# One attention kernel without softmax: TensorE's loop enlarged by a turn and put into one aligned block of program, stores reordered behind loads

## The chip, the cores and the metric

The kernel runs on one core of a Trainium2 chip. The metric is the device time of one execution in microseconds (us); lower is better. The time before is a median of three runs. A separate execution of the same kernel was taken with the hardware profiler, and its rows are what the prediction reads.

## The reference

Linear attention with a ReLU feature map. Q, K and V have 8 batches, 12 heads, 512 positions and 64 channels in float32.

```python
Q_feat = np.maximum(0, Q)
K_feat = np.maximum(0, K)
KV = np.einsum('bhkd,bhkv->bhdv', K_feat, V)
K_sum = np.sum(K_feat, axis=2)
numerator = np.einsum('bhqd,bhdv->bhqv', Q_feat, KV)
denominator = np.einsum('bhqd,bhd->bhq', Q_feat, K_sum)
out = numerator / (denominator[:, :, :, None] + 1e-10)
```

Each head needs a small 64x64 matrix KV and a vector K_sum, and every query row is multiplied with both. Three tensors of 12.58 MB are read and one of the same size is written.

## The kernel before, in words

The 96 heads are worked on in twelve groups of eight ("octets", `NO = 12`). One octet of Q, K or V is 1 MB in float32: 128 partitions with 32 rows of 64 numbers each, contiguous in HBM.

**Loads.** K and V of octet 0 come as float32 over the queues of SP and ACT (L94, L95) into `k8` and `v8`, which are the first two output buffers. Everything else is loaded by POOL (L96, L109), whose transfers turn float32 into bf16 on the way. K and V have a ring of `RING = 6` slots, Q has seven. Loads of octets 1 to 6 are issued at once; from octet 7 on POOL waits until the slot is free (`PR1`, `VC` and `STG`, L104 to L107).

**Stores.** An octet's result is written as float32 into one of `NOUT` buffers `o_sb` and stored by POOL (`store`, L114 to L117) once `NRM1` says that both halves are ready. Octets 10 and 11 are stored by SP. `HEAD = 4` sets how many stores stand between the loads in POOL's order: store 0 is issued ahead of the loads of octet 10, store 1 ahead of those of octet 11, and stores 2 to 9 behind all loads. Each store has a semaphore of its own, and at the end SP waits for all twelve and clears the semaphores (L317 to L321).

**Compute.** DVE prepares K (ReLU times a mask, L237) and V (L241, with ACT's share at L208), two halves g = 0 and 1 of an octet in `prep`, and copies Q (`stage`, L247). TensorE runs one `turn` for each octet, inside a loop (`Fori`, L189): it transposes Q (L158, sixteen), multiplies K with V (L167, 64 products), transposes the octet before back into rows (`back`, L148, sixteen in two halves), forms the denominators (L176) and the numerators (L184). The back transposes of an octet thus stand in the next turn, and those of octet 11 follow the loop as two more calls of `back` (L191 to L193). The loop's first instruction is aligned to the start of a block of 256 instruction slots by `head_slot` (L189). ACT applies ReLU to the transposed Q (L214), moves KV out of PSUM (L219) and the numerators (L228). DVE ends an octet with the denominators (L265 to L273) and `norm` (L259), which multiplies by the reciprocals and writes the output buffer.

**Order of DVE.** In pass o of its loop (L304 to L314): `prep(o+1, 0)`, `stage(o+1)`, `norm(o-1)`, `denominators(o)`, `prep(o+1, 1)`. The last `norm` follows the loop. Before the loop it makes masks and the columns of ones of `vo` with 18 memsets and three reductions (L275 to L300).

**Start.** Three barriers of all engines come ahead of the kernel's own text: one from the construction of the program (profile line L334) and two at L16 (`tc.close()` and `tc.compile()`). The first DMAs are issued behind the last one.

Of the kernel before, what the change touches and what calls it, by code (L numbers as in the profile page):

```python
# [5 lines left out]
def kernel(  # L6
# [5 lines left out]
):  # L12
    nc = tc.nc

    tc.close()
    tc.compile()  # L16

    B, H, S, D = Q.shape
    assert D == 64
    P = 128  # L20
    D1, D4 = D + 1, D + 4
    R = S * 4 // P
    RQ = 2 * R
    U = RQ // 2
    NO = B * H // 8
    assert NO * 8 == B * H and R == 16
    RING = 6
    NOUT = 9
    RUNS = (1,) * 11
    HEAD = 4  # L30

    fp32 = mybir.dt.float32
    bf16 = mybir.dt.bfloat16
    Act = mybir.ActivationFunctionType
    Alu = mybir.AluOpType
    PE, PL, VE, AC, SP = nc.tensor, nc.gpsimd, nc.vector, nc.scalar, nc.sync

    def view(X):
        return X.rearrange("b h s d -> (b h s d)").rearrange("(n p f) -> n p f", p=P, f=RQ * D)

    Qr, Kr, Vr, Or = view(Q), view(K), view(V), view(out)

    def sb(name, shape, dt):
        return nc.alloc_sbuf_tensor(name, shape, dt)[:]
# [3 lines left out]
    def sems(*names):  # L48
        new = [nc.alloc_semaphore(n) for n in names]
        handles.extend(new)  # L50
        return new

    ident = sb("ident", [P, P], bf16)
    ident32 = sb("ident32", [P, P], fp32)
    mask_k = sb("mask_k", [P, 2], fp32)
    mask_v = sb("mask_v", [P, 2], fp32)
    mask_h = sb("mask_h", [P, 8, 2], fp32)
    k_all = sb("k_all", [P, RING, RQ, D], bf16)
    v_all = sb("v_all", [P, RING, RQ, D], bf16)
    q_all = sb("q_all", [P, RING + 1, U * P], bf16)  # L60
    o_sb = [sb(f"o_sb{i}", [P, RQ, D], fp32) for i in range(NOUT)]
    k8, v8 = o_sb[0], o_sb[1]
# [1 line left out]
    q_sb = sb("q_sb", [P, U, P], bf16)  # L64
    qt_sb = sb("qt_sb", [P, U, P], bf16)
    kf = [sb(f"kf{i}", [P, R, 2, D], bf16) for i in range(2)]
    vo = [sb(f"vo{i}", [P, R, 2, D4], bf16) for i in range(2)]
    kvd = sb("kvd", [P, 8, 2 * D1], bf16)
    ot = sb("ot", [P, U, 8, 16], fp32)
    own = sb("own", [P, U, 8, 2], fp32)  # L70
# [10 lines left out]
    ID, STG, PR0, PR1, DEN, NRM0, NRM1, DV = sems(  # L81
        "id", "stg", "pr0", "pr1", "den", "nrm0", "nrm1", "dv")
    VC, KVD, OT = sems("vc", "kvd", "ot")
    CQ0, CQ1, CK0, CK1, CB0, CB1, CD, CO0, CO1 = sems(
        "cq0", "cq1", "ck0", "ck1", "cb0", "cb1", "cd", "co0", "co1")
    landed = {}
    stored = sems(*[f"st{o}" for o in range(NO)])

    def land(name):
        landed[name], = sems(name)  # L90
        return landed[name]
# [7 lines left out]
    def slot(o):  # L99
        return (o - 1) % RING if o > 0 else RING  # L100

    def load(o, n):
        last, to = o + n - 1 - RING, slot(o)
        for X, tile_, c, freed in ((Kr, k_all, "k", [PR1]), (Vr, v_all, "v", [VC, PR1]), (Qr, q_all, "q", [STG])):  # L104
            if last > 0:
                for s in freed:
                    PL.wait_ge(s, last + 1)  # L107
            t = tile_ if c == "q" else tile_.rearrange("p n r d -> p n (r d)")
            PL.dma_start(out=t[:, to:to + n], in_=X[o:o + n].rearrange("n p f -> p n f"),  # L109
                         single_packet=True).then_inc(land(f"{c}{o}"), 16)  # L110
        for i in range(o, o + n):
            run_of[i] = o

    def store(eng, o):  # L114
        eng.wait_ge(NRM1, o + 2)
        kw = {"single_packet": True} if eng is PL else {}
        eng.dma_start(out=Or[o], in_=o_sb[(o + 2) % NOUT].rearrange("p r d -> p (r d)"), **kw).then_inc(stored[o], 16)  # L117

# [4 lines left out]
    o, done = 1, 0  # L123
    for n in RUNS:
        while done < o + n - 1 - RING - HEAD + 1:
            store(PL, done)
# [11 lines left out]
    def arrived(eng, c, o):  # L138
        s = landed[f"{c}{run_of[o]}"]
        if (eng.engine, s.num) not in seen:  # L140
            seen.add((eng.engine, s.num))
            eng.wait_ge(s, 16)

    def back(j):
        for v in range(8):
            t = PE.transpose(ps_o[j][:, P * v:P * v + P], ot[:, 8 * j + v].rearrange("p h c -> p (h c)"), ident32)  # L148
        t.then_inc((CB0, CB1)[j], 1)
# [35 lines left out]
                              start=True, stop=True, skip_group_check=True)  # L185
            t.then_inc((CO0, CO1)[j], 1)

    PE.wait_ge(ID, 4)
    with nc.Fori(1, NO + 1, engines=bass.OrderedEngineSet([PE.engine]), head_slot={PE.engine: 0}) as i:  # L189
        turn(i)  # L190
    PE.wait_ge(OT, NO + 1)  # L191
    back(0)
    back(1)  # L193


    def v_rows(o, g):
        rows = slice(R * g, R * g + R)
        return v_all[:, slot(o), rows] if o > 0 else v8[:, rows]

    def k_rows(o, g):  # L200
        rows = slice(R * g, R * g + R)
        return k_all[:, slot(o), rows] if o > 0 else k8[:, rows]

    def v_scalar(o):
        arrived(AC, "v", o)
        if o == 0:
            AC.wait_ge(ID, 4)
        AC.activation(vo[0][:, :, 1, 2:D + 2], v_rows(o, 0), Act.Copy, scale=mask_v[:, 1:2]).then_inc(VC, 1)  # L208

    v_scalar(0)  # L210
    for o in range(NO):
        for j in range(2):
# [4 lines left out]
        for s in range(2):  # L217
            for c in range(2):
                t = AC.copy(  # L219
                    kvd[64 * c:64 * c + 64, s::2, c * D1:c * D1 + D1].rearrange("p (g t) d -> p g t d", t=2),  # L220
                    ps_kv[64 * s:64 * s + 64, :, 0:2 * (D + 2)].rearrange(
                        "p g (t d) -> p g t d", t=2)[:, :, :, c:c + D1])
# [3 lines left out]
        for j in range(2):  # L226
            AC.wait_ge((CO0, CO1)[j], o + 1)
            t = AC.copy(ot[:, :, 4 * j:4 * j + 4],  # L228
                        ps_o[j].rearrange("p (h u c) -> p u h c", h=4, u=U))
        t.then_inc(OT, 1)  # L230


    def prep(o, g):

        arrived(VE, "k", o)
        for s in range(2):
            VE.tensor_scalar(kf[g][:, :, s, :], k_rows(o, g), scalar1=0.0,  # L237
                             scalar2=mask_k[:, s:s + 1], op0=Alu.max, op1=Alu.mult)
        arrived(VE, "v", o)
        for t in range(1 + g):  # L240
            x = VE.tensor_scalar(vo[g][:, :, t, 2:D + 2], v_rows(o, g), scalar1=mask_v[:, t:t + 1],  # L241
                                 scalar2=None, op0=Alu.mult)
        x.then_inc((PR0, PR1)[g], 1)
# [5 lines left out]
    def norm(o):  # L249
        dst = o_sb[(o + 2) % NOUT]  # L250
        if o >= NOUT:
            VE.wait_ge(stored[o - NOUT], 16)
        VE.wait_ge(DV, 2 * o + 2 + DV0)
        if o == NOUT - 1:
            VE.wait_ge(VC, 1)
        for j in range(2):
            rs = slice(R * j, R * j + R)
            VE.wait_ge((CB0, CB1)[j], o + 2)
            VE.tensor_tensor(dst[:, rs], ps_o[j].rearrange("p (r d) -> p r d", d=D),  # L259
                             rec[o % 2][:, rs].unsqueeze(2).to_broadcast([P, R, D]),  # L260
                             op=Alu.mult).then_inc((NRM0, NRM1)[j], 1)

    def denominators(o):
# [7 lines left out]
                         op=Alu.add, axis=mybir.AxisListType.X).then_inc(DV, 1)  # L271
        VE.wait_ge(DV, 2 * o + 1 + DV0)
        VE.reciprocal(rec[o % 2], den).then_inc(DV, 1)  # L273

    for t in range(2):  # L275
        VE.memset(mask_v[:, t:t + 1], 0.0)
    VE.memset(kvd.rearrange("p h d -> p (h d)").bitcast(fp32), 0.0)
    VE.memset(ot.rearrange("p u h c -> p (u h c)"), 0.0).then_inc(OT, 1)
    ones = [vo[g][:, :, :, 1:D4 - 1][:, :, :, 0:D + 2:D1] for g in range(2)]
    VE.memset(ones[0], 0.0)  # L280
    VE.memset(ones[1], 0.0).then_inc(DV, 1)
    VE.wait_ge(DV, 1)
    for t in range(2):
        for half in range(2):
            b = 64 * half + 32 * t
            VE.memset(mask_v[b:b + 32, t:t + 1], 1.0)
            for g in range(2):
                VE.memset(ones[g][b:b + 32, :, t], 1.0)
    VE.wait_ge(ID, 2)
    VE.tensor_copy(ident32, ident).then_inc(ID, 1)  # L290
    VE.wait_ge(ID, 3)
    for c in range(2):
        VE.tensor_reduce(out=mask_h[:, :, c], in_=ident32.rearrange("p (h b) -> p h b", h=8),
                         op=Alu.add, axis=mybir.AxisListType.X)
    VE.tensor_reduce(out=mask_k, in_=ident32.rearrange("p (t s b) -> p s t b", t=4, s=2),
                     op=Alu.add, axis=mybir.AxisListType.XY).then_inc(ID, 1)
    DV0 = 1
    VE.wait_ge(ID, 4)
    for s in (DEN, NRM0, NRM1):
        VE.sem_inc(s, 1)  # L300
    prep(0, 0)
    prep(0, 1)
    stage(0)
    for o in range(NO):  # L304
        if o + 1 < NO:
            VE.wait_ge(CK0, o + 1)
            prep(o + 1, 0)
            stage(o + 1)
        if o > 0:
            norm(o - 1)  # L310
        denominators(o)
        if o + 1 < NO:
            prep(o + 1, 1)
    norm(NO - 1)  # L314


    for s in stored:  # L317
        SP.wait_ge(s, 16)
    used = sorted(s.num for s in handles)
    assert used == list(range(used[0], used[-1] + 1))  # L320
    SP.sem_clear(range(used[0], used[-1] + 1))  # L321
# [28 lines left out]
```

## Time and profile before

| what | us |
|---|---|
| median of three runs (124.69, 124.86, 125.21) | 124.86 |
| the profiled execution, its own time | 124.66 |
| its span | 123.4 |
| busy: DVE, PE, ACT, POOL | 89.3, 87.4, 79.4, 27.5 |
| first DMA issue (SP, L94) | 1.40 |
| last Q landed | 98.50 |
| last store issued (SP, L117) | 116.7 |
| HBM read and written | 37.75 MB and 12.58 MB |

The span runs from the first instruction of the program to the last, and the profiled execution's own time is 1.3 us longer than its span. Durations below come from this one execution. A loading DMA is counted with the bytes that it writes (bf16), half of what it reads. "PEclk" and the granted clock are the share of TensorE's full speed that the throttle granted. DMA shares over 1.00 are overlapping packets of one DMA engine.

### The profile page before, as it was taken

What the parts mean: (1) busy time and instruction counts of PE and PEld (TensorE: products, weight loads), DVE (VectorE), ACT (ScalarE), POOL (GpSimd) and SP (SyncE); (2) the same over time, 40 slices, a digit from 0 to 9 for tenths busy, and PEclk for the clock granted to TensorE, in tenths of its full rate; (3) what the DMA queues carried; (4) which work ended last, traced back from release to release, by engine and by line L of the source; (5) the groups of instructions that cost most, each with busy time, mean ns of one, the idle gap of its engine ahead of it and who ended that gap; (6) DMA issues with size and microseconds to landing.
All of it is one profiled execution on the core that took longest, in us unless ns stands there. A gap on an engine that the chain in (4) does not pass through costs nothing.

```text
span 123.4 us, 3380 instructions
## 1 busy us (share of the span) xinstructions
PE 87.4 (71%) x1456; PEld 75.9 (62%) x1456; DVE 89.3 (72%) x178; ACT 79.4 (64%) x109; POOL 27.5 (22%) x50
## 2 busy tenths in 40 slices
PE   0000099998998979799897998979449939977400
PEld 0000099986886868688686877958429928947200
DVE  3737906599989899998989989897395497091600
ACT  0043063999988888898888889888539649542000
POOL 3999500050240804309101001010010001000000
PEclk9999999999999999999999999999985995996775
DMA  3999999999999999999999999999999999999994
GB/s 43 369 344 217 213 213 213 213 215 213 214 213 213 213 215 213 214 214 217 214 213 214 213 214 221 371 217 214 375 222 214 343 425 428 425 422 433 420 425 170
DMA packets 6918, 32.57 MB, mean 264 GB/s; under 512 B 768, under 2 KB 768, under 8 KB 5120
## 3 DMA queue, kind: packets, MB, share of 16 engines
q0 software_dynamic: 6336, 28.31, 92.2%
q1 hardware_dynamic: 432, 3.15, 6.6%
q10 hardware_dynamic: 144, 1.05, 2.2%
q8 instruction: 2, 0.03, 0.1%
q14 instruction: 4, 0.03, 0.1%
HBM read 37.75 MB, written 12.58 MB: 408 GB/s over the span
## 4 chain that ended last, share of the span: by engine, by line
DMA 34%; issue 27%; POOL 18%; PE 8%; DVE 5%; ACT 1%; POOLq 0%; DVEq 0%
DMA q_all<-in_Q_dram 34%; POOL k_all L109 6%; POOL q_all L109 5%; POOL v_all L109 5%; DVE o_sb L259 5%; PE ps_o L148 4%; PE ps_kv L167 2%; PE ps_q L158 1%; PE ps_o L184 1%; POOL out_dram L117 1%; ACT ot L228 1%; POOL q_all L96 1%; POOL ident L121 0%; POOL ident L119 0%; POOLq L107 0%
## 5 line engine op out<-in xcount | busy, mean ns | idle before, releaser
L259 DVE TENSOR_TENSOR o_sb<-ps_o,rec 128x1024 f32<-128x1024 f32 x24 | 28.3, 1219 | 7.0 <-PE ps_o L148 6.7
L228 ACT COPY ot<-ps_o 128x1024 f32<-128x1024 f32 x24 | 24.2, 1013 | 10.3 <-PE ps_o L184 9.2
L167 PE MATMUL ps_kv<-vo,kf 64*128 64x132 bf16 x768 | 28.6, 230 | 0.7
L148 PE MATMUL ps_o<-ident,ot 128*128 128x128 f32 x208 | 27.1, 286 | 1.1 <-ACT ot L228 1.1
L167 PEld LDWEIGHTS ps_kv<-vo,kf 64*128 64x128 bf16 x768 | 24.8, 100 | 3.8 <-DVE vo L241 2.3
L214 ACT ACTIVATE qt_sb<-ps_q 128x1024 bf16<-128x1024 bf16 x24 | 23.4, 1030 | 5.1 <-PE ps_q L158 5.1
L158 PE MATMUL ps_q<-ident,q_sb 128*128 128x128 bf16 x192 | 15.3, 243 | 15.4 <-DVE q_sb L247 15.4
L148 PEld LDWEIGHTS ps_o<-ident,ot 128*128 128x128 f32 x208 | 23.8, 146 | 2.7 <-ACT ot L228 1.4
L158 PEld LDWEIGHTS ps_q<-ident,q_sb 128*128 128x128 bf16 x192 | 13.2, 110 | 16.7 <-DVE q_sb L247 15.4
L219 ACT CAST kvd<-ps_kv 64x260 bf16<-64x260 f32 x48 | 18.0, 375 | 7.8 <-PE ps_kv L167 7.4
L184 PE MATMUL ps_o<-qt_sb,kvd 128*128 128x256 bf16 x96 | 15.0, 282 | 10.8 <-DVE o_sb L259 9.8
L237 DVE TENSOR_SCALAR kf<-k_all,mask_k 128x1024 bf16<-128x1024 bf16 x44 | 18.3, 459 | 5.6 <-PE ps_kv L167 5.4
L184 PEld LDWEIGHTS ps_o<-qt_sb,kvd 128*128 128x128 bf16 x96 | 7.7, 100 | 15.6 <-DVE o_sb L259 15.0
L241 DVE TENSOR_SCALAR vo<-v_all,mask_v 128x1024 bf16<-128x1024 bf16 x33 | 15.0, 483 | 0.9 <-DMA v_all<-in_V_dram 0.9
L109 POOL DMA_DIRECT2D k_all<-in_K_dram x11 | 8.4, 763 | 32.1 <-DVE vo L241 32.0
L117 POOL DMA_DIRECT2D out_dram<-o_sb x10 | 5.3, 533 | 40.7 <-DVE o_sb L259 40.7
L208 ACT ACTIVATE vo<-v_all,mask_v 128x1024 bf16<-128x1024 bf16 x11 | 12.7, 1155 | 0.3
L247 DVE COPY q_sb<-q_all 128x2048 bf16<-128x2048 bf16 x12 | 8.3, 694 | 5.7 <-DMA q_all<-in_Q_dram 5.7
L109 POOL DMA_DIRECT2D q_all<-in_Q_dram x11 | 8.9, 811 | 0.0
L109 POOL DMA_DIRECT2D v_all<-in_V_dram x11 | 7.6, 687 | 0.0
L176 PE MATMUL ps_q<-kvd,qt_sb 128*128 128x16 bf16 x192 | 6.9, 180 | 0.0
L176 PEld LDWEIGHTS ps_q<-kvd,qt_sb 128*128 128x128 bf16 x192 | 6.7, 96 | 0.2
(24 smaller groups left out, 27.8 us busy)
## 6 DMA issues: line engine op xcount, KB each, us to landing
out_dram<-o_sb POOLq DMA_DIRECT2D x10, 1024.0 KB, 39.8
q_all<-in_Q_dram POOLq DMA_DIRECT2D x12, 512.0 KB, 36.7
k_all<-in_K_dram POOLq DMA_DIRECT2D x11, 512.0 KB, 33.1
v_all<-in_V_dram POOLq DMA_DIRECT2D x11, 512.0 KB, 34.8
out_dram<-o_sb SPq DMA_DIRECT2D x2, 1024.0 KB, 8.4
o_sb<-in_K_dram SPq DMA_DIRECT2D x1, 1024.0 KB, 8.5
o_sb<-in_V_dram ACTq DMA_DIRECT2D x1, 1024.0 KB, 8.8
```

The source lines that it names most:

```text
L109: PL.dma_start(out=t[:, to:to + n], in_=X[o:o + n].rearrange("n p f -> p n f"), single_packet=True).then_inc(land(f"{c}{o}"), 16)
L148: t = PE.transpose(ps_o[j][:, P * v:P * v + P], ot[:, 8 * j + v].rearrange("p h c -> p (h c)"), ident32)
L158: t = PE.transpose(dst[:, u], q_sb[:, j * (U // 2) + u], ident)
L167: t = PE.matmul(ps_kv[:, half, 0:2 * (D + 2)].rearrange("p (t d) -> p t d", t=2), kf[g][rows, r].rearrange("p s d -> p (s d)"), vo[g][rows ...
L176: t = PE.matmul(ps_den[:, u], qt_sb[:, u], kvd[:, :, 0:2 * D1:2 * D1 - 1], start=True, stop=True, skip_group_check=True)
L184: t = PE.matmul(ps[:, h], kvd[:, 4 * j + h, 1:2 * D + 1], q[:, :, 4 * j + h, :], start=True, stop=True, skip_group_check=True)
L214: AC.activation(qt_sb[:, j * (U // 2):(j + 1) * (U // 2)], ps_q[j].bitcast(bf16).rearrange("p (u f) -> p u f", u=U // 2), Act.Relu)
L219: t = AC.copy(kvd[64 * c:64 * c + 64, s::2, c * D1:c * D1 + D1].rearrange("p (g t) d -> p g t d", t=2), ps_kv[64 * s:64 * s + 64, :, 0:2 * ...
L228: t = AC.copy(ot[:, :, 4 * j:4 * j + 4], ps_o[j].rearrange("p (h u c) -> p u h c", h=4, u=U))
L237: VE.tensor_scalar(kf[g][:, :, s, :], k_rows(o, g), scalar1=0.0, scalar2=mask_k[:, s:s + 1], op0=Alu.max, op1=Alu.mult)
L241: x = VE.tensor_scalar(vo[g][:, :, t, 2:D + 2], v_rows(o, g), scalar1=mask_v[:, t:t + 1], scalar2=None, op0=Alu.mult)
L259: VE.tensor_tensor(dst[:, rs], ps_o[j].rearrange("p (r d) -> p r d", d=D), rec[o % 2][:, rs].unsqueeze(2).to_broadcast([P, R, D]), op=Alu. ...
```

## The change

- TensorE's program is aligned to a block of 256 slots by an `addr_align` ahead of the two barriers of L16, instead of by `head_slot` at its loop. Where padding results, the loader lets the engine branch over it.
- The loop has thirteen turns. The thirteenth takes the place of the two calls of `back` behind the loop; it does everything else of a turn too, on old data, and nobody uses those results. To release its waits, DVE raises `STG`, `PR0` and `PR1` once more behind its last `denominators`, and ACT `KVD` and `VC` behind its last copy.
- `NOUT` goes from 9 to 11 and `HEAD` from 4 to 5: store 0 stands ahead of the loads of octet 11, and all others behind the loads.
- POOL's waits ahead of loads become one for K, one for V and none for Q.
- DVE's set-up of masks and ones uses reductions of the identity and one broadcast copy instead of memsets; semaphores that started at 1 by `sem_inc` now get that from set-up instructions. `norm` waits for the reciprocal only in octet 11; the second copy of V in `prep` waits for the reciprocal of the octet before.
- Stores share semaphores: `ALL` for those of octets 1 to 9, `LAST` for 10 and 11. SP waits for three semaphores at the end, one of them TensorE's `CO1` of the thirteenth turn.

```diff
+    nc.tensor.addr_align(256, offset=0, max_nops=0)
     tc.close()
     tc.compile()
...
-    NOUT = 9
+    NOUT = 11
     RUNS = (1,) * 11
-    HEAD = 4
+    HEAD = 5
...
-    vo = [sb(f"vo{i}", [P, R, 2, D4], bf16) for i in range(2)]
+    vo_all = sb("vo", [P, 2, R, 2, D4], bf16)
+    vo = [vo_all[:, i] for i in range(2)]
...
-    stored = sems(*[f"st{o}" for o in range(NO)])
+    ALL, LAST = sems("all", "last")
+    stored = [sems(f"st{o}")[0] if o + NOUT < NO else ALL if o < NO - 2 else LAST for o in range(NO)]
...
-        for X, tile_, c, freed in ((Kr, k_all, "k", [PR1]), (Vr, v_all, "v", [VC, PR1]), (Qr, q_all, "q", [STG])):
-            if last > 0:
-                for s in freed:
-                    PL.wait_ge(s, last + 1)
+        for X, tile_, c, freed in ((Kr, k_all, "k", PR1), (Vr, v_all, "v", VC), (Qr, q_all, "q", None)):
+            if last > 0 and freed:
+                PL.wait_ge(freed, last + 1)
...
-    PE.wait_ge(ID, 4)
-    with nc.Fori(1, NO + 1, engines=bass.OrderedEngineSet([PE.engine]), head_slot={PE.engine: 0}) as i:
+    with PE.Fori(1, NO + 2) as i:
         turn(i)
-    PE.wait_ge(OT, NO + 1)
-    back(0)
-    back(1)
...
         if o == 0:
-            AC.wait_ge(ID, 4)
+            AC.wait_ge(ID, 5)
...
+    AC.wait_ge(KVD, NO)
+    AC.wait_ge(VC, NO)
+    AC.sem_inc(KVD, 1)
+    AC.sem_inc(VC, 1)
...
         for t in range(1 + g):
+            if t and o:
+                VE.wait_ge(DV, 2 * o + DV0)
...
-        VE.wait_ge(DV, 2 * o + 2 + DV0)
+        if o == NO - 1:
+            VE.wait_ge(DV, 2 * o + 2 + DV0)
...
-    for t in range(2):
-        VE.memset(mask_v[:, t:t + 1], 0.0)
-    VE.memset(kvd.rearrange("p h d -> p (h d)").bitcast(fp32), 0.0)
+    VE.memset(kvd.rearrange("p h d -> p (h d)").bitcast(fp32), 0.0).then_inc(DEN, 1)
...
-    ones = [vo[g][:, :, :, 1:D4 - 1][:, :, :, 0:D + 2:D1] for g in range(2)]
-    VE.memset(ones[0], 0.0)
-    VE.memset(ones[1], 0.0).then_inc(DV, 1)
-    VE.wait_ge(DV, 1)
-    for t in range(2):
-        for half in range(2):
-            b = 64 * half + 32 * t
-            VE.memset(mask_v[b:b + 32, t:t + 1], 1.0)
-            for g in range(2):
-                VE.memset(ones[g][b:b + 32, :, t], 1.0)
...
-    for c in range(2):
-        VE.tensor_reduce(out=mask_h[:, :, c], in_=ident32.rearrange("p (h b) -> p h b", h=8),
-                         op=Alu.add, axis=mybir.AxisListType.X)
+    VE.tensor_reduce(out=mask_v, in_=ident32.rearrange("p (a t b) -> p t a b", a=2, t=2),
+                     op=Alu.add, axis=mybir.AxisListType.XY).then_inc(ID, 1)
     VE.tensor_reduce(out=mask_k, in_=ident32.rearrange("p (t s b) -> p s t b", t=4, s=2),
-                     op=Alu.add, axis=mybir.AxisListType.XY).then_inc(ID, 1)
-    DV0 = 1
+                     op=Alu.add, axis=mybir.AxisListType.XY).then_inc(NRM0, 1)
+    VE.tensor_reduce(out=mask_h, in_=ident32.rearrange("p (h b) -> p h b", h=8).unsqueeze(2).to_broadcast([P, 8, 2, 16]),
+                     op=Alu.add, axis=mybir.AxisListType.X).then_inc(NRM1, 1)
     VE.wait_ge(ID, 4)
-    for s in (DEN, NRM0, NRM1):
-        VE.sem_inc(s, 1)
+    VE.tensor_copy(vo_all.rearrange("p g r t d -> p (g r) t d")[:, :, :, 1:D4 - 1][:, :, :, 0:D + 2:D1],
+                   mask_v.unsqueeze(1).unsqueeze(3).to_broadcast([P, 2 * R, 2, 2])).then_inc(ID, 1)
+    DV0 = 0
+    VE.wait_ge(ID, 5)
...
+    for s in (STG, PR0, PR1):
+        VE.wait_ge(s, NO)
+        VE.sem_inc(s, 1)
     norm(NO - 1)
...
-    for s in stored:
-        SP.wait_ge(s, 16)
+    SP.wait_ge(CO1, NO + 1)
+    SP.wait_ge(ALL, 16 * (NOUT - 2))
+    SP.wait_ge(LAST, 32)
```

## The prediction

> **What bounds the kernel now.** I read the page's slices first, because they show whether one resource is full all the way.
>
> ```profile
> PE 87.4 (71%) x1456; PEld 75.9 (62%) x1456; DVE 89.3 (72%) x178; ACT 79.4 (64%) x109; POOL 27.5 (22%) x50
> DMA  3999999999999999999999999999999999999994
> GB/s 43 369 344 217 213 213 213 213 215 213 214 213 213 213 215 213 214 214 217 214 213 214 213 214 221 371 217 214 375 222 214 343 425 428 425 422 433 420 425 170
> ```
>
> The DMA engines are full in 38 of 40 slices; no compute engine is above 72%. 213 GB/s are bf16 bytes written, so 426 GB/s of fp32 read, the same as the 425 of the stores. The page's 37.75 MB read and 12.58 MB written take 50.33 / 0.426 = 118.1 us. That leaves 5.3 us of the 123.4 us span, at the two ends. So I asked for the stages at both ends (columns: stretch, its length, busy time of PE, weight loads, DVE, ACT and POOL, granted clock, DMA share, GB/s).
>
> ```profile
> 2.00:2.40 0.40, 0.00 (x0) 0.00 (x0) 0.13 (x1) 0.00 (x0) 0.40 (x1) 1.00 0.00 0
> 2.40:3.00 0.60, 0.00 (x0) 0.00 (x0) 0.49 (x1) 0.00 (x0) 0.41 (x2) 1.00 1.61 218
> 119.00:120.00 1.00, 0.00 (x0) 0.00 (x0) 0.00 (x0) 0.00 (x0) 0.00 (x0) 0.50 1.09 459
> 120.00:121.00 1.00, 0.00 (x0) 0.00 (x0) 0.00 (x0) 0.00 (x0) 0.00 (x0) 0.50 0.99 418
> 121.00:122.00 1.00, 0.00 (x0) 0.00 (x0) 0.00 (x0) 0.00 (x0) 0.00 (x0) 0.50 0.39 164
> 122.00:123.40 1.40, 0.00 (x0) 0.00 (x0) 0.00 (x0) 0.00 (x0) 0.00 (x0) 0.50 0.07 29
> ```
>
> Data flows from 2.4 us on. After 121.0 only 0.39 + 1.4 x 0.07 = 0.49 us of work per engine is left, so an even split would end at 121.5. By the packet rows of the trace the last byte leaves at 122.71: twelve engines end between 121.20 and 121.58, four at 122.2 to 122.7. 0.65 us later (the last landing, SP's clear) the span ends.
>
> Why four are late is read from the queue list and the packet rows.
>
> ```profile
> q8 instruction: 2, 0.03, 0.1%
> q14 instruction: 4, 0.03, 0.1%
> ```
>
> These six packets are program text, fetched while the kernel runs: 16 KB at 11.50 and 114.34 us (0.94 and 0.97 us each), 8 KB at 32.75, 49.66, 97.46 and 105.55 (0.31 to 0.32). The sixteen landing marks of each transfer show what they do. Octet 0's Q lands within 0.28 us. The next load after 11.50, octet 1's K, has fifteen marks within 0.33 and one at 1.37, and one engine stays that late up to the last load. Store 2, after 97.46, has two late ones (1.30 and 1.52), store 5 a third (0.83 growing to 1.0), and store 11 four: 1.13, 1.15, 1.49, 1.59 behind the first. The 8 KB fetches of the load phase add only 0.25 to 0.5. Every engine carries an equal share and never catches up, so the last one sets the end.
>
> Each fetch follows, by some 3.85 us, an engine's step into a new stretch of program: TensorE's jump into its loop (ends 7.66, fetch 11.50) and its leaving it (110.36 to 114.34); DVE's records 59 and 187, counted from 0 and exactly 128 apart (28.8 and 93.65); ACT's record 46 (45.7); and the point where POOL waits at its last store and steps beyond (101.5 to 101.8).
>
> Last, the chain, to see how late the last store may be.
>
> ```profile
> 56.48 42.02 DMA q_all<-in_Q_dram
> ...
> 110.17 0.63 PE ps_o L184 x4
> 110.80 0.02 issue
> 110.82 1.02 ACT ot L228
> 111.84 0.04 issue
> 111.89 3.50 PE ps_o L148 x16
> 115.39 0.02 issue
> 115.41 1.23 DVE o_sb L259
> ```
>
> The last Q lands at 98.50; 18.2 us of compute follow; SP issues store 11 at 116.7. It needs 1.0 us to its first packet (as at the start: issued 1.40, first packet 2.41) and one transfer is 2.45 us (distance of landings in a row). The other stores keep the engines busy to 121.5 - 2.45 = 119.0. So the last store is hidden if issued before 118.0.
>
> **The change, part by part.** The sum is against the profiled execution: 124.66 us, span 123.4, 1.3 outside. The median, 124.86, is 0.20 higher.
>
> Order of transfers: no byte is added. Today stores 0 and 1 precede the last six loads (store 0 lands before K of octet 10, store 1 before K of octet 11); with HEAD = 5 only store 0 does, ahead of octet 11. Octets 10 and 11 land one transfer earlier, 2.46 us, Q of octet 11 at 96.0. DVE can follow: it waits 2.14 us for Q of octet 10 (at 88.67) today, and an octet costs it 6.9 of 7.3 us. Norm 11 now waits for store 0, landed by 89: nothing. Stores 1 to 9 queue behind the last load on POOL with no wait that is not long met, save for the last ones as today. Eleven buffers: nothing further. Sum 0 on the DMA, -2.46 on the compute chain.
>
> Thirteenth turn: the last transposes back (L148) now stand behind sixteen of Q and 64 products of K and V. The stretches at full clock give 0.87 us (L158) and 2.18 us (L167), 3.05 in all. They start once DVE has let STG, PR0 and PR1 go to 13, behind its last reciprocal (111.3 - 2.46 = 108.8), and ACT VC; before, the same point waited for ACT's copy, to 111.84 - 2.46 = 109.4. So the transposes back start at 108.8 + 3.05 = 111.85 instead of 111.89 today, in the same half-clock stretch: last store at 116.6, unchanged, 1.4 us inside its cover. Cost 0; without that cover each us would be one us. What of turn 13 comes after norm 11 lies beside the last store, and SP waits for CO1 long before the landing.
>
> Program text: DVE loses 17 records of set-up (31 to 14) and ten of its twelve waits ahead of norm, and gains three: 210 to 186, so record 187, whose fetch was at 97.46, is not reached. POOL loses five waits (L107), 68 to 63, and ends before its step at 68. TensorE has no code behind its loop, and enters its block ahead of the second barrier, near 0.8 us, so that the fetch at 11.50 comes before data flow. The four late engines come to the level of the twelve: 122.71 - 121.58 = 1.13 us off. Bounds: 0 (a fetch remains at the end) to 1.5 (122.71 - 121.20); I take 1.13, since every late mark answers to one of these four fetches. [...]
>
> The start: TensorE's padding ahead of its aligned block is jumped over between the first and second barrier, and it is the last to arrive there (rows of the barriers; columns: engine's sequencer, count, ns, first and last start).
>
> ```profile
> L16 PEldq DRAIN  x2: 8/8/8, 0.8 to 1.2; - x2
> L189 PEldq COMPARE_BRANCH  x13: 76/208/309, 7.3 to 110.3; - x13
> ```
>
> The jump into the loop, today's nearest row, took 0.31 us, and 0.13 passed to the next instruction, against 0.1 between instructions without one: +0.3 us on every transfer. Below, 0 (POOL is not ready at the barrier before 0.74 anyway); above, a fetch waited for (a rival). I take 0.3: it is the same jump of the same engine.
>
> DVE's shorter set-up: 0, DVE then waits 2.75 us for K at 9.97. ACT's wait for the fifth ID: 0, its table is loaded by 8.6 and V lands at 10.15. The second copy of V's wait for the reciprocal three instructions before: 0 to 0.05 an octet, hidden by the loads. SP's fewer waits: the last one still ends at the landing, 0.
>
> Sum: 124.66 + 0.3 - 1.13 = 123.83; with 0.20 to the median, 124.0 us.
>
> **The rivals.**
>
> One late fetch remains. DVE's end (186) is one record short of its step, and what runs behind the kernel's text may cross at once; TensorE's, behind a body that nearly fills a block, likewise; or the early fetch falls into the first packets and delays its engine for good. One engine 1.05 us late ends at 122.3 to 122.6 by the marks: 0.1 to 0.4 off, eaten by the 0.3 of the start. 124.7 to 125.1, no change. For it: POOL's fetch at 105.55 came from leaving its program. Against: ACT left its program at 111.84 and nothing was fetched for it. 0.30. Or fetches cost nothing, and four engines are late for another reason: 124.86 + 0.3 = 125.2, also no change. 0.05. [...]
>
> The jump finds its block not loaded: slower. Place: TensorE between the two barriers, with the three issuing engines waiting. Price: from 1.0 + 0.9 = 1.9 us (idle DMA: the start's first packet and the fetch's length) to 3.85 + 0.94 = 4.8 us (as under load), in place of 0.3: 125.6 to 128.5. It decides from a jump of 1.75 us (123.73 without the 0.3, and 125.48). Against: the jump to the loop at 7.35 fetched nothing first, so its block was there then. For: nothing shows that it was there at 0.7. [...] 0.13.
>
> Turn 13 uncovers the last store. With its work at half clock (1.91 for L158, 3.1 for L167 by its first half at 103.9 to 105.4) it is issued near 118.7; alone on the engines it ends as late as today. Issue at t ends at t + 1.0 + 2.45 + 0.65 + 1.3 + 0.2, so it is slower by 0.62 us only from t = 119.9: 125.5. 0.04.
>
> **How the numbers follow.** A measurement of this kernel can tell some 0.5%, 0.62 us, from no change: 124.24 to 125.48. Forecast, 0.45, all of it faster. Unchanged: the two cases of 0.30 and 0.05. Slower: 0.13 + 0.04, and 0.03 for what I do not see. The range: below, 124.0 - 0.3 (no cost at the start) - 0.37 (1.5 saved instead of 1.13) = 123.3; above, it takes in the unchanged cases, the uncovered store and the cheapest unloaded jump, 125.9. The forecast's own range is 123.3 to 124.3.
>
> **What would show it.** Right: no 16 KB fetch after 3 us, no fetch after 90; octet 1's K landing within 0.5 us; the last store's marks within 0.6; the last Q landing near 96.3; 80 more matmuls ahead of the last L148; store 11 issued at 116 to 118. Wrong: first packet later than 3 us (the jump); one mark of store 11 a us behind (a fetch left); DMA share under 0.9 before 120 us (the last store uncovered).

## The result, and the profile after

The changed kernel takes 125.28 us (median of nine runs, 125.18 to 125.82); the kernel before, on the same chip, 124.80. The ratio is 1.0046, 95% interval 1.0031 to 1.0062: 0.5 us slower, where 124.0 had been forecast. The profiled execution after took 125.47 us with a span of 123.5; over the nine runs the medians of span and of the time outside it are 123.8 and 1.50. The rows below thus come from the execution with the shortest span of the nine and the longest time outside it.

The page of the changed kernel, its slices and its queues:

```profile
DMA  1899999999999999999999999999999999999994
GB/s 27 316 359 235 214 212 214 218 214 212 216 215 214 214 212 212 214 212 212 214 212 212 215 212 215 212 216 320 279 214 285 427 427 422 422 422 427 424 430 191
...
q8 instruction: 1, 0.02, 0.0%
q14 instruction: 2, 0.02, 0.0%
```

The DMA engines are still full from the third slice on. The first slice moves 27 GB/s instead of 43: the data starts later, with its first packet at 2.82 us instead of 2.41. Three packets of program text are left of six: 16 KB at 2.23 us, 8 KB at 43.12 and 50.15. Nothing is fetched between 51 us and the end of the span, as forecast.

The start, from the rows of lines 16 and 18 of the changed kernel, the jump and the barriers (columns: the sequencer, operation, count, shortest, median and longest ns, first and last start):

```profile
L16 PEldq COMPARE_BRANCH  x1: 309/309/309, 0.8 to 0.8; - x1
```

```profile
L18 PEldq DRAIN  x2: 8/37/66, 1.2 to 1.6; - x2
```

and from the timeline (start, length):

```profile
1.82 0.38 SPq L99 DMA_DIRECT2D o_sb<-in_K_dram  x1
1.82 0.39 ACTq L100 DMA_DIRECT2D o_sb<-in_V_dram  x1
```

TensorE's jump, at the line of the `addr_align`, takes 0.31 us, its arrival at the barrier moves from 0.8 to 1.2, and every first DMA issue from 1.40 to 1.82.

The end of the chain that ended last (start, length, what):

```profile
56.90 39.12 DMA q_all<-in_Q_dram
96.02 0.02 issue
...
108.22 1.07 PE ps_q L164 x16
109.29 2.00 PE ps_kv L173 x64
111.29 1.04 PE ps_o L154 x8
...
112.45 2.37 DVE o_sb L269 x2
```

The last Q lands at 96.02 instead of 98.50. The thirteenth turn's transposes of Q and products of K and V now stand ahead of the last transposes back, 3.07 us of them. The last store is nevertheless issued at 114.84 instead of 116.67, for the most part because TensorE's half-clock stretches fell elsewhere (98.4 to 101.8 and from 118.9 on): the last sixteen transposes back took 1.97 us instead of 3.49.

What the end of the span looks like, by stages (length; busy time of PE, weight loads, DVE, ACT, POOL; granted clock; DMA share; GB/s):

```profile
119.00:120.00 1.00, 0.00 (x0) 0.00 (x0) 0.00 (x0) 0.00 (x0) 0.00 (x0) 0.50 1.02 434
120.00:121.00 1.00, 0.00 (x0) 0.00 (x0) 0.00 (x0) 0.00 (x0) 0.00 (x0) 0.50 0.97 410
121.00:122.00 1.00, 0.00 (x0) 0.00 (x0) 0.00 (x0) 0.00 (x0) 0.00 (x0) 0.50 0.74 311
122.00:123.50 1.50, 0.00 (x0) 0.00 (x0) 0.00 (x0) 0.00 (x0) 0.00 (x0) 0.50 0.05 22
```

After 121.0 there are 0.74 + 1.5 x 0.05 = 0.82 us of work per engine, so an even split would end at 121.8; the last byte leaves at 122.84. Of the sixteen marks of store 11 (the increments of its semaphore; each load and each store has sixteen in the trace, and that each is the share of one DMA engine is my reading, since the trace names no engine), fourteen lie within 0.79 us of the first, two are 1.28 and 1.54 behind it. The tail is still uneven by 1.0 us.

### The profile page after: what moved, and what is told of

It is laid out like the page before. It is cut to its first block, busy times and chain, and to the rows that moved or that the text cites. A ratio compares the mean times of both kernels' runs of the same rounds, so it can differ in the third digit from the quotient of the medians.

```text
span 123.5 us, 3560 instructions
## 1 busy us (share of the span) xinstructions
PE 88.1 (71%) x1560; PEld 76.1 (62%) x1560; DVE 88.0 (71%) x163; ACT 79.3 (64%) x109; POOL 27.5 (22%) x50
## 3 DMA queue, kind: packets, MB, share of 16 engines
q1 hardware_dynamic: 432, 3.15, 6.4%
## 4 chain that ended last, share of the span: by engine, by line
DMA 39%; DVE 27%; PE 23%; issue 2%; POOL 1%; DVEq 0%
DMA q_all<-in_Q_dram 32%; DVE o_sb L269 13%; PE ps_kv L173 10%; DMA o_sb<-in_K_dram 8%; PE ps_o L154 7%; PE ps_q L164 4%; DVE kf L244 4%; DVE vo L250 4%; PE ps_o L190 2%; DVE den L280 2%; DVE own L275 1%; DVE rec L283 1%; DVE q_sb L256 1%; POOL k_all L114 1%; POOL v_all L114 0%
## 5 line engine op out<-in xcount | busy, mean ns | idle before, releaser
L173 PE MATMUL ps_kv<-vo,kf 64*128 64x132 bf16 x832 | 29.3, 222 | 0.9
L154 PE MATMUL ps_o<-ident,ot 128*128 128x128 f32 x208 | 25.6, 276 | 0.0
L154 PEld LDWEIGHTS ps_o<-ident,ot 128*128 128x128 f32 x208 | 22.5, 141 | 1.4
L190 PE MATMUL ps_o<-qt_sb,kvd 128*128 128x256 bf16 x104 | 16.1, 280 | 9.5 <-DVE o_sb L269 8.8
L190 PEld LDWEIGHTS ps_o<-qt_sb,kvd 128*128 128x128 bf16 x104 | 8.3, 100 | 14.8 <-DVE o_sb L269 13.1
L114 POOL DMA_DIRECT2D k_all<-in_K_dram x11 | 7.3, 660 | 32.5 <-DVE vo L250 32.3
L182 PE MATMUL ps_q<-kvd,qt_sb 128*128 128x16 bf16 x208 | 7.5, 180 | 0.0
L182 PEld LDWEIGHTS ps_q<-kvd,qt_sb 128*128 128x128 bf16 x208 | 7.3, 96 | 0.2
L114 POOL DMA_DIRECT2D q_all<-in_Q_dram x11 | 6.9, 630 | 0.0
```

The lines of the kernel that those rows point to most:

```text
L173: t = PE.matmul(ps_kv[:, half, 0:2 * (D + 2)].rearrange("p (t d) -> p t d", t=2), kf[g][rows, r].rearrange("p s d -> p (s d)"), vo[g][rows ...
L182: t = PE.matmul(ps_den[:, u], qt_sb[:, u], kvd[:, :, 0:2 * D1:2 * D1 - 1], start=True, stop=True, skip_group_check=True)
L190: t = PE.matmul(ps[:, h], kvd[:, 4 * j + h, 1:2 * D + 1], q[:, :, 4 * j + h, :], start=True, stop=True, skip_group_check=True)
```

## The experiments

Theory A, formed from these rows: the end is the engines' mean plus the lateness of the one that is latest, so that one late engine costs what four do; the jump costs its whole 0.4 us; and the fetch that was moved to the start still makes an engine late. All runs at a glance. "K late" is how far the worst of the sixteen marks of octet 1's K lies behind their mean; span and the time outside it are medians over the runs, the other columns are of the profiled execution. All times in us.

| kernel | first issue | 16 KB fetches | K late | last store issued | span | outside | time | against before |
|---|---|---|---|---|---|---|---|---|
| before | 1.40 | 11.50, 114.34 | 1.15 | 116.67 | 123.5 | 1.3 | 124.8 | |
| after | 1.82 | 2.23 | 0.88 | 114.84 | 123.8 | 1.50 | 125.28 | 1.0046 (1.0031 to 1.0062) |
| e1_jump_late | 1.39 | 5.19 | 1.62 | 115.45 | 123.45 | 1.48 | 124.95 | 1.0008 (0.9987 to 1.0028) |
| e2_jump_alone | 1.82 | 1.89, 113.99 | 0.80 | 115.24 | 124.4 | 1.33 | 125.73 | 1.0081 (1.0050 to 1.0112) |
| e3_old_order | 1.82 | 1.89 | 1.87 | 118.63 | 124.1 | 1.56 | 125.65 | 1.0078 (1.0048 to 1.0108) |
| e4_long_texts | 1.82 | 1.86 | 0.83 | 115.75 | 123.75 | 1.33 | 125.10 | 1.0030 (1.0012 to 1.0049) |
| e5_late_long | 1.40 | 9.94 | 1.14 | 114.95 | 123.4 | 1.33 | 124.73 | 0.9992 (0.9981 to 1.0004) |
| e6_late_short | 1.39 | 9.12 | 1.42 | 114.07 | 123.45 | 1.47 | 124.94 | 1.0007 (0.9997 to 1.0018) |
| e7_one_engine | 1.39 | 10.12 | 2.05 | 116.25 | 124.4 | 1.30 | 125.70 | 1.0069 (1.0053 to 1.0084) |
| e8_old_order_late | 1.39 | 10.50 | 1.45 | 118.01 | 123.5 | 1.32 | 124.83 | 1.0002 (0.9986 to 1.0018) |
| e10_dve_long | 1.39 | 10.27 | 1.23 | 114.60 | 123.35 | 1.50 | 124.84 | 1.0006 (0.9988 to 1.0024) |
| e11_twelve_turns | 1.39 | 10.12, 111.19 | 1.23 | 112.52 | 123.3 | 1.33 | 124.67 | 0.9978 (0.9958 to 0.9997) |

The kernel before took 124.76 to 124.80 in these comparisons; its span and outside time were 123.5 and 1.30 to 1.32 in each.

**The jump, taken back.**

```diff
-    nc.tensor.addr_align(256, offset=0, max_nops=0)
...
-    with PE.Fori(1, NO + 2) as i:
+    with nc.Fori(1, NO + 2, engines=bass.OrderedEngineSet([PE.engine]), head_slot={PE.engine: 0}) as i:
```

> The changed kernel with the aligned block entered at the loop again, behind all three barriers, instead of between the first and the second. Theory A (the jump of TensorE between the barriers holds back every DMA, and one late DMA engine sets the end): first DMA issue back from 1.82 to 1.40 us, the 16 KB fetch near 2.8 us and still one engine a us late, so 0.4 us faster than the changed kernel: 124.7 to 124.95, no change against before. Rival B (the start is hidden; what costs is the thirteenth turn or the moved stores): no gain, 125.2 to 125.3. Rival C (the early fetch is what costs, and a later one would cost more): 125.5 or more.

```profile
1.39 0.38 SPq L98 DMA_DIRECT2D o_sb<-in_K_dram  x1
1.40 0.39 ACTq L99 DMA_DIRECT2D o_sb<-in_V_dram  x1
```

The timeline has the first issue back at 1.39, and the time falls to 124.95, 0.33 below the changed kernel; the span falls by 0.35. The jump stood on the path of the transfers, as theory A has it; rival B, no gain, is refuted. The fetch did not come at 2.8 us but at 5.19, in the middle of the first loads, and left its engine 1.62 us late, more than either kernel has.

**The jump alone, in the kernel before.**

```diff
+    nc.tensor.addr_align(256, offset=0, max_nops=0)
     tc.close()
     tc.compile()
...
-    with nc.Fori(1, NO + 1, engines=bass.OrderedEngineSet([PE.engine]), head_slot={PE.engine: 0}) as i:
+    with PE.Fori(1, NO + 1) as i:
```

> The kernel before with nothing but the aligned block entered between the first and second barrier; twelve turns and the two calls of back behind the loop as before. Theory A: first DMA 0.42 us later, 124.8 + 0.4 = 125.2; the fetch at 11.5 moves to 2.2 us, those at 97 to 114 stay, and one engine is late either way. Rival B: 124.8, as the start is hidden. Rival C: under 124.6, as the fetch at 11.5 is gone.

Slower by 0.97 us, more than any theory said. The start accounts for 0.42. In the profiled execution one mark of store 9 is 2.67 us behind the mean and one of store 11 is 1.85 behind (1.13 in the kernel before), as if two fetches had met on one engine; the trace does not name engines, so this is argued, not shown. What is shown is that moving the fetch from 11.5 to 1.9 us gains nothing. The 0.55 us beyond the start stay unexplained.

**Old order of stores, thirteen turns.**

```diff
-    NOUT = 11
+    NOUT = 9
-    HEAD = 5
+    HEAD = 4
```

> The changed kernel with NOUT = 9 and HEAD = 4, so that stores 0 and 1 stand between the loads as before and the thirteenth turn stays. Theory A: last store issued 2.4 us later (114.9 to 117.3), still under the other stores, which end near 119.5: within 0.2 us of the changed kernel, 125.1 to 125.5. Rival B (the moved stores cost something by themselves): 124.8 to 125.0. Rival C (the order is needed, the tail opens): 126 or more.

125.65, above theory A's range and below rival C's. It does not decide: in this run the early fetch hit harder (1.36 us long instead of 0.93) and one engine was 1.87 us late from the first load on. So the order was tried again without the early fetch, below.

**Long programs again.**

```diff
+    pad = sb("pad", [P, 32], fp32)
+    for n in range(24):
+        VE.memset(pad[:, n:n + 1], 0.0)
...
+    padp = sb("padp", [P, 8], fp32)
+    for n in range(5):
+        PL.memset(padp[:, n:n + 1], 0.0)
```

> The changed kernel with 24 idle memsets more in DVE's set-up and 5 more in POOL's, so that both programs are again as long as before (210 and 68 records) and the fetches near 97 and 105 us come back; they hide behind the wait for K. Theory A (one late engine sets the end, and there is one already): two more engines about 1 us late, time up by 0.0 to 0.2 us: 125.3 to 125.5. Rival of the prediction (each such fetch removed takes its own part off the end): 125.9 to 126.4.

The queues of this kernel's page:

```profile
q14 instruction: 4, 0.03, 0.1%
q8 instruction: 1, 0.02, 0.0%
```

Two fetches came back, at 95.17 and 103.44 us, and the marks of store 11 have three late engines again (0.75, 1.18 and 1.21 behind the mean). The span did not move: 123.75 against 123.8. The rival (0.6 us or more slower) is refuted: with an engine late already, these two fetches cost nothing. The time even fell by 0.18, all of it outside the span, 1.33 instead of 1.50. No theory had expected that.

**Late entry, with long and with short programs.** From e1_jump_late; e5 with the padding of e4, e6 without.

```diff
+    PE.wait_ge(ID, 5)
     with nc.Fori(1, NO + 2, engines=bass.OrderedEngineSet([PE.engine]), head_slot={PE.engine: 0}) as i:
```

> The changed kernel with the aligned block entered at the loop, and only after DVE's set-up (a wait for ID = 5, so the 16 KB fetch falls into the steady flow near 10 to 12 us, as before), and with DVE's and POOL's programs padded to their old length. Theory A (the end is the mean of the engines plus the lateness of one; a fetch among the first packets makes an engine 0.9 to 2.0 us late, one in the steady flow 1.05 to 1.15; short programs move a fetch behind the span): last store's mark mean 121.9, worst 1.15 later, 1.3 outside the span: 124.4 to 124.7. Rival B (only the start of the data counts, the lateness does not): like e1_jump_late, 124.9 to 125.0.

> As e5_late_long, but with the short programs of the changed kernel. Theory A: the fetches near 95 and 103 us go, the span is the same within 0.1, and the time outside the span grows from 1.3 to 1.5 or more: 0.1 to 0.3 us slower than e5_late_long. Rival of the prediction (fewer fetches, earlier end): 0.3 us or more faster than e5_late_long.

e5_late_long has its fetch at 9.94 and takes 124.73 us, just above theory A's range: 0.2 better than e1_jump_late, of which 0.15 lies outside the span; the lateness at the end was 1.34, not 1.15. e6_late_short has neither of the two fetches of DVE and POOL and the same span (123.45 against 123.4), and 0.14 more outside it. The rival, that fewer fetches end earlier, is refuted for the second time.

**One of the two programs short.** From e5_late_long.

```diff
-    padp = sb("padp", [P, 8], fp32)
-    for n in range(5):
-        PL.memset(padp[:, n:n + 1], 0.0)
```

> e5_late_long with POOL's program short again (63 records) and DVE's still long (210). It tells which short program puts time behind the span (1.33 us in e5_late_long, 1.47 in e6_late_short). If DVE's, whose 186 records end one short of its step at record 187: 1.33 outside, 124.6 to 124.8. If POOL's: 1.47 or more outside, 124.85 to 125.0. On either theory the span is 123.4 within 0.1, although the fetch near 103 us is gone; the rival of the prediction (each fetch costs at the end) has the span 0.3 or more shorter.

1.50 outside, in every one of the twelve runs between 1.44 and 1.54, against 1.27 to 1.35 in e5_late_long and 1.26 to 1.44 for the kernel before beside it. So it is POOL's program: five records fewer on POOL, and 0.17 us more behind the span. With 63 records (the changed kernel, e1, e3, e6) nothing is fetched between 52 us and the end of the span; with 68 a fetch came at 105.55 in the kernel before and at 103.44 in e4. Three of the five traces of kernels with a short POOL program (the changed kernel at 125.26 us, e3_old_order at 125.73, e6_late_short at 125.20) show an 8 KB fetch behind the span, and e1_jump_late and this kernel show none; that this fetch is POOL's, and that it makes the cost, is argued.

**One engine loaded by hand.** From e5_late_long.

```diff
+    EXTRA, = sems("extra")
+    for n in range(8):
+        SP.dma_start(out=o_sb[10][n:n + 1].rearrange("p r d -> p (r d)"), in_=Kr[0][n:n + 1]).then_inc(EXTRA, 16)
```

> e5_late_long plus eight more transfers of one row of 8 KB (64 KB in all, 0.13% of the bytes), issued by SP at the start into an output buffer that is not yet in use; a transfer of one row is a single piece of work for one DMA engine. Theory A: if all eight go to one engine, that engine has 8 x 0.305 = 2.4 us more to do and ends 2.4 to 2.7 us behind the mean, unless it is the fetch's own engine (then 3.5): 1.3 to 2.4 us slower than e5_late_long. Rival (the engines share one pool of bandwidth): 64 KB at 426 GB/s, 0.15 us.

SP issues the eight from 1.83 us on, in 2.50 us. DVE also waits for them ahead of octet 8's `norm`, which starts at 89.28 in the kernel before. The row of the eight in the issues of the page (count, size):

```profile
o_sb<-in_K_dram SPq DMA_DIRECT2D x8, 8.0 KB
```

The end of the span by stages, in e5_late_long and then in this kernel:

```profile
121.00:122.00 1.00, 0.00 (x0) 0.00 (x0) 0.00 (x0) 0.00 (x0) 0.00 (x0) 0.50 0.36 148
122.00:123.00 1.00, 0.00 (x0) 0.00 (x0) 0.00 (x0) 0.00 (x0) 0.00 (x0) 0.50 0.08 33
```

```profile
121.00:122.00 1.00, 0.00 (x0) 0.00 (x0) 0.00 (x0) 0.00 (x0) 0.00 (x0) 0.50 0.43 180
122.00:123.00 1.00, 0.00 (x0) 0.00 (x0) 0.00 (x0) 0.00 (x0) 0.00 (x0) 0.50 0.14 57
123.00:124.40 1.40, 0.00 (x0) 0.00 (x0) 0.00 (x0) 0.00 (x0) 0.00 (x0) 0.50 0.03 12
```

64 KB more, 0.13% of the bytes, cost 0.97 us, 0.8%. Every load from octet 1's K on has one mark 2.05 to 2.27 us behind the mean, beside another at 1.1, as late as the fetch's engine in e5_late_long, and store 11's worst is 2.02 behind instead of 1.34. After 122 us the DMA share is 0.14 and 0.03, and 0.14 x 16 is work for about two of the sixteen engines. The shared pool of the rival would have cost 0.15. The size fell short of the 1.3 that I had set as theory A's least: the late mark is 2.02 us behind at store 11 after up to 2.27 at the loads, and the kernel it is compared with ends with an engine 1.34 late itself. That the eight went to one engine is read from the packets and the marks: SP's queue has 448 packets instead of 432, one of data and one of completion for each, and one mark of sixteen lies 2 us behind the mean while fourteen stay together.

**Old order of stores, without the early fetch.** From e5_late_long, NOUT = 9 and HEAD = 4.

> e5_late_long with NOUT = 9 and HEAD = 4, that is with thirteen turns and the old order of stores, without the chance of the early fetch that e3_old_order had. Theory A: last store issued near 117.5 to 118.5 instead of 115 to 116, at the edge of its cover: mean of the last store's marks up by 0 to 0.3, time up by 0 to 0.4 us. Rival C (the tail opens for good): 1 us or more. Rival B (moved stores cost by themselves): 0.2 or more faster.

Last store issued at 118.01, 3.1 us later than in e5_late_long, and the time 124.83 against 124.73: within its noise. The other stores cover it. The order of stores and the buffers are worth 0.1 us or nothing.

**Twelve turns.** From e5_late_long, with the end of TensorE's program as before and without the releases of the thirteenth turn.

```diff
-    with nc.Fori(1, NO + 2, engines=bass.OrderedEngineSet([PE.engine]), head_slot={PE.engine: 0}) as i:
+    with nc.Fori(1, NO + 1, engines=bass.OrderedEngineSet([PE.engine]), head_slot={PE.engine: 0}) as i:
         turn(i)
+    PE.wait_ge(OT, NO + 1)
+    back(0)
+    back(1)
...
-    SP.wait_ge(CO1, NO + 1)
```

> e5_late_long with twelve turns and the two calls of back behind the loop, as before the change; the order of stores stays changed. Theory A: last store issued some 2 us earlier (115 to 113), which buys nothing, since other stores cover it; the fetch near 110 to 114 us comes back and makes one more engine 1.1 us late, beside one that is: 124.65 to 125.0, within 0.3 us of e5_late_long. Rival (the thirteenth turn is on the path): 0.5 us or more faster than e5_late_long. Rival of the prediction (the last fetch costs on its own): 0.5 us or more slower.

The second 16 KB fetch is back at 111.19 and the last store goes out at 112.52, and the time is 124.67, 0.06 from e5_late_long. Neither the turn nor its fetch is on the path. This is the fastest of the kernels tried, 0.2% below the kernel before at an interval that ends at 0.9997, which among ten experiments is no proof of a gain; it keeps the changed order of stores and set-up, and gives up the early block, the thirteenth turn and the short programs.

## Why the prediction was wrong

**The program text, -1.13: the step that failed.** The fetches went as worked out: DVE has 186 records and POOL 63, and none of the four that had left an engine late at the end of the span is where it was. But the term counted the four late engines as if all would vanish, while one of them was only moved, and its ground for that, "every late mark answers to one of these four fetches", does not hold in the changed kernel (below). The block entered near 0.8 us has its fetch at 2.23 to 3.15, and the first data packets leave at 2.82; octet 1's K then has its worst mark 0.88 us behind the mean (1.25 behind the first), and an engine stays that late until the last load. The span gives the measured size: 123.8 - 123.5 - 0.42 for the start = -0.1 us instead of -1.13. The marks of store 11 in the two profiled executions say the same without that subtraction: their mean moved from 121.99 to 122.30 us, and the latest lies 1.01 us behind it instead of 1.13. The mean fits too, as an estimate: the three fetches that are gone took 0.97 + 0.31 + 0.31 = 1.6 us, 0.1 us for each of sixteen engines, and 0.42 - 0.1 is 0.32.

e4, e6, e10 and e11 show why the term is worth so little: each of the three later fetches, taken out or put back, left the span the same within 0.1 us while another engine was late. That one engine with more to do does cost is shown by e7 (0.97 us for 64 KB). Only e2 may speak the other way, with its 0.55 us that no run explains.

Which engine is the last in the changed kernel stays open. The engine that the early fetch left behind may be it. But in the four kernels that fetch nothing between 52 us and the end of the span (the changed kernel, e1, e3 and e6) the second latest mark goes from 0.35 to 0.41 us behind the mean at the last Q to 0.70 to 1.11 at store 11, so an engine falls behind in the store phase without a fetch. In none of the twelve kernels is store 11's latest mark less than 0.93 behind its mean, and none runs without a 16 KB fetch, so no run tells how level the end would be without one.

The first rival had the early fetch as its third cause, with a chance of 0.30; "delays its engine for good" is what the marks show up to the last load (0.88 us behind the mean at octet 1's K, 0.80 at the last Q), but its 124.7 to 125.1 us missed the time. The rival with a chance of 0.05, four engines late for another reason, came nearest with 125.2, and the store phase bears it out in part; that its number came so near is partly luck: it lacks the 0.2 us outside the span and takes the start at 0.3.

The step "the fetch at 11.50 comes before data flow" was wrong by 0.3 us of overlap. With the lag that the prediction itself read from the rows, 3.85 us, the fetch would have come near 5 us, among the first loads, and no reason was given for an earlier one; it came 1.1 us behind the jump. And, as e4 shows, even a fetch that is over at 2.79 ahead of a first packet at 2.83 goes with an engine 0.83 us late at that K. How an early fetch does that is open. The lag itself is less sure than the prediction has it: the rows have DVE's records 59 and 187 start at 30.23 and 95.84 and ACT's record 46 at 46.59, not at 28.8, 93.65 and 45.7, so 3.85 us is read from TensorE's two cases and POOL's alone.

**The start, +0.3.** Right in kind and place; it measured 0.42; e1 took 0.33 of the time back, and the span of e5 is 0.35 below that of e4, which has the same long programs and the early jump. The size was off by the drain behind the jump: it starts 0.36 us later than before (1.19 against 0.83) and takes 66 ns instead of 8, which makes 0.42. The jump waited for no fetch (it took 0.31 us, and the block's fetch came at 2.23), so the rival of the block that is not loaded did not occur, and no run here shows one.

**Outside the span, 1.3 taken as fixed.** It grew to 1.50. No term of the sum stood for it, and e10 ties it to the short program of POOL, the edit that I had counted as a gain. Start, tail and this part make 0.42 - 0.1 + 0.2 = 0.5 us, the measured difference; since the tail's -0.1 is what is left of the span, this sum closes by itself.

**The order of stores and the thirteenth turn, 0 together.** Right. The last Q came 2.5 us earlier, the turn put 3.07 us ahead of the last transposes (3.05 forecast), and what the last store gained or lost lay under the other stores: 112.52 to 118.01 as its issue, with times between 124.67 and 124.83 (e11, e5, e8). That it was issued at 114.84 and not at 116.6 comes mainly from the clock, which was forecast at half for the last transposes and was full (granted 1.00 from 110 to 116 us).

**DVE's shorter set-up and SP's fewer waits, 0.** Right: with both of them and without the jump (e6), the span is that of the kernel before within 0.05 us.

**The marks that were to show it.** No fetch late in the span: right. Octet 1's K within 0.5 us and store 11 within 0.6: wrong, 1.25 and 1.54. A mark of store 11 a us behind, the sign of a fetch left, came, but with no late fetch. First packet later than 3 us: it was 2.82, on the right side.

## What to carry to other kernels

When a kernel is bound by its DMA engines, look at the spread of one transfer's landing marks. Here the last byte left at 122.84 us where an even split would end at 121.8; with three of four late fetches gone the tail gained 0.1 us while a mark as late was left (1.01 us behind the mean at store 11, 1.13 before); and the fetch moved from 11.50 to 2.23 us still went with a mark 0.88 us late. What delays the first DMA issue was paid nearly in full here: a jump of 0.3 us on an engine that merely had to arrive at a barrier put every first issue 0.42 us later, and 0.33 to 0.35 us came back without it. Shortening a program is not a gain by itself; compare the time outside the span too (1.50 us in e10_dve_long against 1.33 in e5_late_long).

## What the runs showed that I had not expected

- A program that is shorter on POOL made the time outside the span longer: 1.47 to 1.56 us with 63 records (five kernels), 1.30 to 1.33 with 68.
- With the 16 KB fetch at 1.86 to 5.19 us, near the first packets, one mark of octet 1's K was 0.80 to 1.87 us late, with one kernel differing from another; with the fetch in the steady flow (9.12 to 11.50) it was 1.14 to 1.45 (the kernel before, e5, e6, e8, e10 and e11).
- In the store phase a second engine falls 0.7 to 1.1 us behind the mean without any fetch (the changed kernel's marks from 109 us on; e1, e3 and e6 alike). Its cause is open.
